# More seven-product quads in the down and output products of a float32 transformer block

## The chip, the core and the metric

The kernel runs on one core of a Trainium2 chip. Its time is the device time of one execution in microseconds; "before" is the median of three runs, 2025.66 us (2025.6 to 2025.71). The engines of the core run side by side, each with its own queue of instructions: TensorE (PE in the profile, its weight loads PEld), VectorE (DVE), ScalarE (ACT), GpSimd (POOL) and SyncE (SP), which here issues most loads. They wait for each other through semaphores.

## The reference

A block on 256 tokens of width 2048, in float32: a gated feed-forward block, a mixer (a recurrent branch and a pooling branch, gated and projected), and a second feed-forward block, each behind a norm and with a residual. What the change touches are the two down products and the mixer's last product:

```python
def _swiglu(x, w_gate, w_up, w_down):
    return (jax.nn.silu(x @ w_gate) * (x @ w_up)) @ w_down      # 256x2048, 2048x5632 twice, 5632x2048

f = _swiglu(_rmsnorm(h, ln_ffn1_pre[l]), ffn1_gate[l], ffn1_up[l], ffn1_down[l])
h = h + MACARON_WEIGHT * _rmsnorm(f, ln_ffn1_post[l])
...
m = jax.nn.sigmoid(g_a) * y_a + jax.nn.sigmoid(g_b) * y_b
return m @ w_out                                                 # 256x2048, 2048x2048
```

## The kernel before

**Products.** Every float32 operand is split into two halves of a faster type: ScalarE casts the value to its high half (H), VectorE subtracts that from the value and gets the low half (L). A product is then three matmuls, H·H, L·H and H·L (`mm3`, L311 to L315). A matmul takes 128 rows of the inner dimension, 128 tokens and 512 columns, and adds into a bank of PSUM. There are two halves of the tokens (h = 0, 1), so a plain step over one row block and one 512-column block is 2 x 3 matmuls. The down products have 44 row blocks and four column blocks, the output product 16 and four.

**Column pairs.** `seven` (L482) makes two neighbouring column blocks at once, f (first) and l (last). An order in letters says what TensorE does in turn: `f` or `l` is a pair, two row blocks against one column block, 12 matmuls (`pair`, L518); `q` is a quad, two row blocks against both column blocks (`quad`, L529). A quad uses Strassen's scheme in Winograd's form: seven products instead of eight, 21 matmuls. Its operands are sums of weight blocks (t13, t2 and t4, on VectorE, L548 to L560) and sums of activations (`sums`, L404, on VectorE and ScalarE; one set serves four row blocks, thus two quads, and is kept for both column pairs). The four weight operands of a quad are two raw ones and two sums; each is cast on ScalarE and has its low half made on VectorE (L562 to L573). When the last quad of a pair is done, its partial results are merged (`merge`, L622: a copy on ScalarE and four adds on VectorE, then one for each half of f, L653, and of l, L665). With `trail`, the last 16 row blocks of the pair's l column are done by halves of the tokens (`by_half`, L385), so that the first half is finished early.

**Buffers.** The weight halves go round in a ring of five buffers each (`WS_BUFS`), raw weights in four (`W32_BUFS`) or in the 33 general units of 4 KB a partition that also hold activations and sums. Four PSUM banks serve f and l, four the products that a quad keeps apart (p1, p5, p6, p7).

**Order.** For the two feed-forward blocks and the output product the order of work is made by a planner in the kernel (`Plan`, L87). TensorE's steps stand in the order of the letters, each at a planned time; every other operation is a node with a cost, a due time worked back from what needs it (L139 to L147), and buffers that it takes and gives back. `solve` (L134) puts the nodes into one sequence by a list scheduling with modelled costs, and `run` (L261) writes them out in it, as each engine's own order, under `manual_schedule` for TensorE, ScalarE, VectorE and SyncE. GpSimd is not in that list; there a scheduler of the framework decides. GpSimd issues the small transfers that carry the activations of the gate and up stage over from its layout to the next one (`carry`, L893; 16 transfers for each of the 11 blocks), the gains, the residual's loads and stores. `fetch` (L356) is the load, cast and low half of a pair.

The orders of the down products (`DOWN`, for columns 0 and 1, then 2 and 3), of the output product (`OUT`: column 0 plain, 1 and 2 as a pair, 3 plain) and of the gate and up products (`GATE_UP`, per block) are L45 to L48.

Of the kernel before, what the change touches and what calls it, by code (L numbers as in the profile page):

```python
# [17 lines left out]
P = 128  # L18
# [68 lines left out]
class Plan:  # L87
# [46 lines left out]
    def solve(s):  # L134
        succ = {n: [] for n in s.nodes}
        for n in s.nodes:
            for d in n.deps:
                succ[d].append(n)
        for n in reversed(s.nodes):  # L139
            for m in succ[n]:  # L140
                if n.eng == "PE":
                    break
                v = m.due - n.dur - (n.lat + (EARLY if m.eng == "PE" else 0.0)
                                     if m.eng != n.eng else 0.0)
                n.due = v if n.due is None else min(n.due, v)
            if n.due is None:
                n.due = n.born + LATEST  # L147
# [67 lines left out]
class Block:  # L215
# [139 lines left out]

    def fetch(s, w, k, c0, keep, hold=False):  # L356

        p, x = s.plan, {}
        src = Tok("w32", "unit")
        dst = [Tok("unit"), Tok("unit")] if hold else [Tok("ring")]  # L360

        def load():
            x["w"] = s.get_w(w, k, 2, c0, 512, own=src.of == "unit")

        def cast():
            x["v"], x["H"], x["L"] = s.halves_of(x["w"], hold)
            s.nc.scalar.copy(x["H"], x["v"])  # L367

        def low():
            s.nc.vector.tensor_tensor(out=x["L"], in0=x["v"], in1=x["H"].bitcast(F32),  # L370
                                      op=ALU.subtract)
            keep([(k + i, x["H"][:, i], x["L"][:, i]) for i in range(2)])
        n = p.op("SP", 0.4, load, take=[src], size=0.52, chain="SP")
        n = p.op("ACT", cost("ACT", 1024), cast, [n], take=dst, chain="cast")
        return p.op("DVE", cost("DVE", 1024), low, [n], rel=[src]), dst
# [28 lines left out]
    def sums(s, T, Td, j, out, own=None, nq=2, used=()):  # L404
# [25 lines left out]
        def parts():  # L430

            for n_ in ("sH", "sL"):
                if j % 2 == 0:
                    own["12" + n_] = s.unit((P, 2, 2, 2, P), F32R, n_)
                if j == 0:
                    own["4" + n_] = s.unit((P, 4, 2, P), F32R, n_)
# [3 lines left out]
            f = tt["f"]  # L440
            tt["p"] = [([u[:, j % 2] for u in s12], f[:, :2]),
                       ([u[:, j] for u in s4], f[:, 3]), (s3, f[:, 2])]
            for (H, _), v in tt["p"]:
# [38 lines left out]
    def seven(s, wf, cf, wl, cl, at, dep, KT, need, sm, order, ev_f, ev_l, used, trail=0):  # L482
# [34 lines left out]

        def pair(k, w, c0, b):  # L518
            low, dst = s.fetch(w, k, c0, keep)

# [8 lines left out]
        def quad(q):  # L529
# [40 lines left out]
            def low(n_, m):  # L570
# [3 lines left out]
            ld = [p.op("SP", 0.4, lambda m=m: get(m), take=([ka], [kb], (), ())[m], size=0.26,  # L574
                       chain="SP") for m in range(4)]

# [58 lines left out]
        for c in order:  # L635
            if c == "q":
                last["q"] = quad(nq)
                nq += 1
                if nq == n:
                    merge(last["q"])  # L640
                    if "f" in m:
                        close_f()
                continue
            w_ = (wf, cf) if c == "f" else (wl, cl)
            last[c] = pair(next(ks[c]), *w_, c)
            left[c] = left.get(c, 0) + 1
# [207 lines left out]
    def carry_steps(s, T1, T, x32=None):  # L854
# [3 lines left out]

        def move():
            if x32 is None:  # L860
                x[0] = s.unit((P, 4, 2, 4, 32), F32, "x32")
            src = s.blocks(T1[0])
            for i in range(4):
                for q in range(4):
# [19 lines left out]
        return move, high, low  # L884

    def carry_now(s, T1, T, x32):
        move, high, low = s.carry_steps(T1, T, x32)
        move()
# [3 lines left out]

    def carry(s, T1, T, turned, k1):  # L893

        p = s.plan
        move, high, low = s.carry_steps(T1, T)
        kx, kT = Tok("unit"), [Tok("unit"), Tok("unit")]
        n = p.op("POOL", 10.0, move, turned, [kx], [k1], chain="carry", spare=2, lat=8.0)
        hs = []
        for h in range(2):  # L900
            hs.append(p.op("ACT", cost("ACT", 512), lambda h=h: high(h), [n] + hs,
                           kT if h == 0 else (), chain="high",
                           spare=KEEP))
        for h in range(2):
            n = p.op("DVE", cost("DVE", 512), lambda h=h: low(h), [hs[h], n], (),
                     [kx] if h else ())
# [35 lines left out]
    def ffn(s, wg, wu, wd, uT, rs, gpost, resid, emit, reload, xs=None):  # L942
        nc = s.nc
        hT, sm = [], [None] * 8
        at = s.T_at(uT)
# [40 lines left out]
        def carry(b, turned, k1):  # L986
            n, k = s.carry(T1[b], hT, turned, k1)
            hTd.append(n)
# [966 lines left out]
```

## Time and profile before

| | |
|---|---|
| Median of three runs | 2025.66 us |
| The profiled execution | 2025.32 us |
| Its span, first to last instruction | 2023.6 us |
| Granted TensorE clock | 0.998 |
| Read from memory | 396.69 MB, 200 GB/s over the span |

In order of time the span holds: gate and up products of the first feed-forward block until about 469 us, its down product to about 701, the mixer with the output product (about 1257 to 1323 for the pair and the trailing column), gate and up products of the second block to about 1783, its down product to about 2013, and the store of the last rows.

The page's section 1 gives busy time by engine; a busy TensorE means that a matmul is in flight, and matmuls overlap, so the distance from start to start is their cost and not the duration of one. The list of waits gives for an engine what ended its idle time before an instruction: total, number of times, longest. Rows of a timeline give the start, the time, the engine, the source line, the operation, out<-in, how many equal ones were merged, and in brackets the idle time before it.

### The profile page before, as it was taken

How to read it: one execution, taken by the hardware profiler on the slowest of the kernel's cores; microseconds unless marked ns; L12 is line 12 of the kernel's file. 1: busy time of each engine (PE TensorE's matmuls, PEld its weight loads, DVE VectorE, ACT ScalarE, POOL GpSimd, SP SyncE). 2: the span in 40 equal slices, each digit the busy share in tenths (PEclk: the TensorE clock that was granted, in tenths of full speed). 3: DMA queues.
4: the chain of work that ended last, by engine and by line, in shares of the span. 5: the costliest groups of instructions: out<-in, count | busy, mean ns of one | idle time of the engine just before them, and what ended most of it. 6: DMA issues, size and time to landing. Idle time of an engine off the chain costs nothing.

```text
span 2023.6 us, 28609 instructions
## 1 busy us (share of the span) xinstructions
PE 2008.3 (99%) x9987; PEld 1660.2 (82%) x9987; DVE 1774.4 (88%) x2344; ACT 1180.8 (58%) x1575; POOL 325.2 (16%) x673
## 2 busy tenths in 40 slices
PE   9999999999999999999999999999999999999997
PEld 7888888888888888888788788888888888888886
DVE  6999999999989857799689577779999999999896
ACT  7565665655655566685576434565566556566553
POOL 0111211121000123403220111011112111210000
PEclk9999999999999999999999999999999999999999
DMA  7757475577567677757456558756574755775674
GB/s 267 254 179 265 148 253 188 186 221 245 185 204 268 225 204 214 204 175 216 147 169 187 160 169 278 245 196 232 187 266 151 246 190 183 223 243 189 203 261 145
DMA packets 227098, 423.55 MB, mean 209 GB/s; under 512 B 24320, under 2 KB 27786, under 8 KB 226954
## 3 DMA queue, kind: packets, MB, share of 16 engines
q1 hardware_dynamic: 204393, 384.70, 58.5%
q0 software_dynamic: 22272, 36.51, 5.5%
q8 instruction: 78, 1.28, 0.3%
q10 hardware_dynamic: 288, 0.52, 0.1%
q14 instruction: 67, 0.54, 0.1%
HBM read 396.69 MB, written 8.39 MB: 200 GB/s over the span
## 4 chain that ended last, share of the span: by engine, by line
PE 98%; issue 1%; DVE 1%; ACT 0%; DMA 0%; DVEq 0%; POOLq 0%; POOL 0%; SPq 0%; ACTq 0%
PE mm L313 27%; PE mm L315 27%; PE mm L314 27%; PE ms L313 4%; PE ms L315 4%; PE ms L314 4%; PE tr L822 0%; PE pA L1673 0%; PE mc L790 0%; PE pU L1769 0%; DMA w<-in_ffn_gate_dram 0%; PE pSa L1781 0%; PE pY L1804 0%; DVE xL L840 0%; PE pT L1840 0%
## 5 line engine op out<-in xcount | busy, mean ns | idle before, releaser
L313 PE MATMUL mm<-wH,xH 128*128 128x512 f32 (+1 forms) x2184 | 851.5, 391 | 0.4 <-ACT xH L831 0.4
L315 PE MATMUL mm<-wH,xL 128*128 128x512 f32 (+1 forms) x2184 | 847.8, 388 | 1.6 <-DVE xL L840 1.6
L314 PE MATMUL mm<-wL,xH 128*128 128x512 f32 (+1 forms) x2184 | 847.5, 388 | 0.0
L367 ACT CAST wH<-w 128x1024 fp32r<-128x1024 f32 x333 | 346.8, 1053 | 239.7 <-PE mm L315 209.2
L315 PEld LDWEIGHTS mm<-wH,xL 128*128 128x128 f32 x2184 | 409.9, 188 | 87.5 <-DVE xL L840 3.2
L313 PEld LDWEIGHTS mm<-wH,xH 128*128 128x128 f32 x2184 | 410.0, 188 | 85.5 <-ACT xH L831 1.0
L314 PEld LDWEIGHTS mm<-wL,xH 128*128 128x128 f32 x2184 | 410.1, 188 | 82.3
L370 DVE TENSOR_TENSOR wL<-w,wH 128x1024 fp32r<-128x1024 f32 x333 | 396.9, 1217 | 39.5 <-ACT wH L367 36.5
L567 ACT CAST wH<-t 128x1024 fp32r<-128x1024 f32 x188 | 198.2, 1054 | 222.8 <-PE mm L315 156.5
L290 DVE TENSOR_TENSOR wL<-w,wH 128x1024 fp32r<-128x1024 f32 (+2 forms) x202 | 239.0, 1192 | 96.5 <-ACT wH L289 93.3
L289 ACT CAST wH<-w 128x1024 fp32r<-128x1024 f32 (+2 forms) x202 | 207.7, 1034 | 164.5 <-PE mm L315 142.9
L865 POOL DMA_DIRECT2D x<-T x352 | 172.5, 498 | 748.4 <-DVE T L848 394.9
L572 DVE TENSOR_TENSOR wL<-t,wH 128x1024 fp32r<-128x1024 f32 x188 | 225.5, 1217 | 14.1 <-ACT wH L567 13.9
L567 ACT CAST wH<-w 128x1024 fp32r<-128x1024 f32 (+1 forms) x188 | 153.6, 835 | 48.4 <-PE mm L315 40.3
L572 DVE TENSOR_TENSOR wL<-w,wH 128x1024 fp32r<-128x1024 f32 (+1 forms) x188 | 175.6, 950 | 2.4 <-ACT wH L567 2.4
L550 DVE TENSOR_TENSOR t<-w,w 128x1024 f32<-128x1024 f32 x94 | 114.4, 1217 | 0.7 <-DMA w<-in_ffn_down_dram 0.7
L313 PE MATMUL ms<-wH,sH 128*128 128x512 f32 x252 | 98.0, 389 | 0.0
L314 PE MATMUL ms<-wL,sH 128*128 128x512 f32 x252 | 98.0, 389 | 0.0
L315 PE MATMUL ms<-wH,sL 128*128 128x512 f32 x252 | 98.0, 389 | 0.0
L559 DVE TENSOR_TENSOR t<-w,t 128x512 f32<-128x512 f32 x94 | 64.8, 689 | 2.1
L555 DVE TENSOR_TENSOR t<-w,t 128x512 f32<-128x512 f32 x94 | 64.3, 684 | 0.8
L619 DVE TENSOR_TENSOR u<-ms,u 128x512 f32<-128x512 f32 x92 | 61.3, 685 | 1.6
(311 smaller groups left out, 2017.6 us busy)
## 6 DMA issues: line engine op xcount, KB each, us to landing
w<-in_w_in_dram SPq DMA_DIRECT2D x128, 512.0 KB
w<-in_ffn_down_dram SPq DMA_DIRECT2D x116, 512.0 KB
w<-in_ffn_up_dram SPq DMA_DIRECT2D x114, 512.0 KB
w<-in_ffn_gate_dram SPq DMA_DIRECT2D x112, 512.0 KB
w<-in_ffn_gate_dram SPq DMA_DIRECT2D x128, 256.0 KB
w<-in_ffn_up_dram SPq DMA_DIRECT2D x124, 256.0 KB
w<-in_ffn_down_dram SPq DMA_DIRECT2D x120, 256.0 KB
w<-in_w_out_dram SPq DMA_DIRECT2D x28, 512.0 KB
```

The costliest lines, as they stand in the source:

```text
L289: s.nc.scalar.copy(vH, v)
L290: s.nc.vector.tensor_tensor(out=vL, in0=v, in1=vH.bitcast(F32), op=ALU.subtract)
L313: nc.tensor.matmul(ps, aH, bH, start=start, stop=False)
L314: nc.tensor.matmul(ps, aH, bL, start=False, stop=False)
L315: nc.tensor.matmul(ps, aL, bH, start=False, stop=stop)
L367: s.nc.scalar.copy(x["H"], x["v"])
L370: s.nc.vector.tensor_tensor(out=x["L"], in0=x["v"], in1=x["H"].bitcast(F32), op=ALU.subtract)
L550: V.tensor_tensor(out=v["t13"], in0=v["a"], in1=v["b"][:, :1].to_broadcast([P, 2, 512]), op=ALU.subtract)
L559: V.tensor_tensor(out=v["t24"][:, 1], in0=v["b"][:, 1], in1=v["t24"][:, 0], op=ALU.subtract)
L567: nc.scalar.copy(H, src)
L572: V.tensor_tensor(out=L, in0=src, in1=H.bitcast(F32), op=ALU.subtract)
L865: nc.gpsimd.dma_start(out=x[0][q * 32:q * 32 + 32, i], in_=src[i * 32:i * 32 + 32, q])
```

## The change

Three lines of letters change: the first pair of a down product has eight quads instead of seven, one in f's part and seven among the l pairs; the last pair has ten instead of eight, and its f and l pairs alternate between them; the output product's pair has four instead of two. GpSimd is added to the engines whose order the planner writes out. The planner's model of transfers changes (a higher rate; GpSimd's transfers no longer share SyncE's line; a transfer's time counts in due times; loads are not planned more than 22 us ahead of their due time), and the carry's 16 transfers become four nodes of four with a longer modelled latency. `sums` lets a fifth set of activation sums have units of its own, and `sm` has room for it.

The diff also brings a second way to make low halves (a copy of the negated high half, and a transfer from memory that adds onto it). It is reached by letters in upper case in an order, of which there are none, and by blocks in `BY_DMA`, which is `range(0)`; so nothing of it is in the built program.

```diff
-DOWN = ((0, "fffffffffqffffqff" "lqlllqllqllqllqlllll", 0),
-        (2, "fffqffqffqffqffqffqf" "lqllqlll", TRAIL))
-OUT = ((0, "", 0), (1, "fffffqf" "lqlllll", 0), (3, "", TRAIL))
+DOWN = ((0, "fffffffffffqfff" "qllqllqllqllqllqllqll", 0),
+        (2, "fqflqfqflqfqflqfqflqfqfqff", TRAIL))
+OUT = ((0, "", 0), (1, "fffqfq" "qlqlll", 0), (3, "", TRAIL))
...
+BY_DMA = range(0)
...
-SOON, LATEST, BEFORE = 22.0, 12.0, 12.0
+SOON, FETCH, LATEST, BEFORE = 22.0, 22.0, 12.0, 12.0
 EARLY = 0.5
-RATE, LEAVE, LAND = 0.25, 1.05, 2.0
+RATE, LEAVE, LAND, ADD, MOVE = 0.28, 1.05, 2.0, 10.0, 12.0
...
         for n in reversed(s.nodes):
+            lat = max(n.lat, n.size and LEAVE + n.size / RATE + LAND)
...
-                v = m.due - n.dur - (n.lat + (EARLY if m.eng == "PE" else 0.0)
+                v = m.due - n.dur - (lat + (EARLY if m.eng == "PE" else 0.0)
...
-                line = max(n.free + LEAVE, line) + n.size / RATE
-                n.end = max(n.end, line + LAND)
+                start = max(n.free + LEAVE, line)
+                line = start + n.size / RATE
+                n.end = max(n.end, (line if n.eng == "SP" else n.free + LEAVE + n.size / RATE)
+                            + LAND)
...
-        with s.tc.manual_schedule(engines={E.PE, E.Activation, E.DVE, E.SP}):
+        with s.tc.manual_schedule(engines={E.PE, E.Activation, E.DVE, E.SP, E.Pool}):
...
-        n = p.op("SP", 0.4, load, take=[src], size=0.52, chain="SP")
+        n = p.op("SP", 0.4, load, take=[src], size=0.52, chain="SP", ahead=FETCH)
...
-                if j % 2 == 0:
+                if j > 3:
+                    u = s.unit((P, 4, 2, P), F32R, n_)
+                    own["12" + n_], own["4" + n_] = u[:, :2], u[:, 2]
+                elif j % 2 == 0:
...
-            kept = [Tok("unit") for _ in range(2 * (j % 2 == 0) + 2 * (j == 0))]
+            kept = [Tok("unit") for _ in range(2 * (j % 2 == 0 or j > 3) + 2 * (j == 0))]
...
-        n = p.op("POOL", 10.0, move, turned, [kx], [k1], chain="carry", spare=2, lat=8.0)
+        n = None
+        for i in range(4):
+            n = p.op("POOL", 2.5, lambda i=i: move(i), [*turned, n], [kx] if i == 0 else (),
+                     [k1] if i == 3 else (), chain="carry", spare=2, lat=MOVE)
...
-        hT, sm = [], [None] * 8
+        hT, sm = [], [None] * 12
```

More of the change, by code (lines that the diff above doesn't have):

```diff
@@ L354, in gemm_tok, with fetch @@
                 evac(h, pss[h])
[L356 to L358 removed]
+    def fetch(s, w, k, c0, keep, hold=False, by_dma=False):
+        nc, p, x = s.nc, s.plan, {}
         src = Tok("w32", "unit")
@@ L516, in keep, with pair @@
             ws.update((k, (wH, wL)) for k, wH, wL in tiles)
-        def pair(k, w, c0, b):
-            low, dst = s.fetch(w, k, c0, keep)
+        def pair(k, w, c0, b, by_dma):
+            low, dst = s.fetch(w, k, c0, keep, by_dma, by_dma)
             def do():
@@ L574, in quad @@
             ld = [p.op("SP", 0.4, lambda m=m: get(m), take=([ka], [kb], (), ())[m], size=0.26,
-                       chain="SP") for m in range(4)]
+                       chain="SP", ahead=FETCH) for m in range(4)]
             def half(n_, m, deps, rel):
@@ L643, in seven @@
                 continue
+            by_dma, c = c in "FL", c.lower()
             w_ = (wf, cf) if c == "f" else (wl, cl)
-            last[c] = pair(next(ks[c]), *w_, c)
+            last[c] = pair(next(ks[c]), *w_, c, by_dma)
             left[c] = left.get(c, 0) + 1
@@ L857, in carry_steps, with move @@
         x, own = [x32], []
-        def move():
-            if x32 is None:
+        def move(*part):
+            if x[0] is None:
                 x[0] = s.unit((P, 4, 2, 4, 32), F32, "x32")
             src = s.blocks(T1[0])
-            for i in range(4):
+            for i in part or range(4):
                 for q in range(4):
@@ L883, in low, with whole, minus, add @@
                                     in1=part(dH, h).bitcast(F32), op=ALU.subtract)
-        return move, high, low
+        def whole(h):
+            nc.scalar.copy(part(own[0][1].bitcast(F32), h), by_k(h))
+        def minus():
+            x[0] = x[0].rearrange("p i h k c -> p (i h k c)")
+            nc.scalar.activation(out=x[0], in_=own[0][0].rearrange("p k t -> p (k t)")
+                                 .bitcast(F32), func=AF.Copy, scale=-1.0)
+        def add():
+            nc.gpsimd.dma_start(out=own[0][1].rearrange("p k t -> p (k t)"), in_=x[0],
+                                accum_op=ALU.add)
+        return move, high, low, whole, minus, add
     def carry_now(s, T1, T, x32):
-        move, high, low = s.carry_steps(T1, T, x32)
+        move, high, low = s.carry_steps(T1, T, x32)[:3]
         move()
@@ L903, in carry @@
                            spare=KEEP))
+        if by_dma:
+            for h in range(2):
+                n = p.op("ACT", cost("ACT", 512), lambda h=h: whole(h), [n, *hs])
+            n = p.op("ACT", cost("ACT", 1024), minus, [n, *hs])
+            return p.op("POOL", 1.25, add, [n], (), [kx], size=0.94, lat=ADD), kT
         for h in range(2):
@@ L986, in carry @@
         def carry(b, turned, k1):
-            n, k = s.carry(T1[b], hT, turned, k1)
+            n, k = s.carry(T1[b], hT, turned, k1, b in BY_DMA)
             hTd.append(n)
```

27 lines of the change are left out of this document (19 added, 8 removed).

## The prediction

> **What bounds the kernel now.** I read the page's head first, then the list of what TensorE waited for, then busy time by stretch.
>
> ```profile
> span 2023.6 us, 28609 instructions
> ...
> PE 2008.3 (99%) x9987; PEld 1660.2 (82%) x9987; DVE 1774.4 (88%) x2344; ACT 1180.8 (58%) x1575; POOL 325.2 (16%) x673
> ...
> PE warm L698 <- POOL ident masks.py:199: 1.7, 1, 1.7
> PE mm L315 <- DVE xL L840: 1.6, 4, 0.5
> PE pS L1789 <- ACT R L1783: 0.7, 1, 0.7
> PE mm L313 <- ACT xH L831: 0.4, 2, 0.2
> ```
>
> TensorE is busy for 2008.3 of 2023.6 us. The four lines behind it are all its waits on other engines, 4.4 us together, and none has a weight operand (wH, wL) in it: every weight half comes in time. So the end moves only if TensorE gets fewer instructions, or if it begins to wait. The second depends on VectorE, which makes the low halves:
>
> ```profile
> 100.00:460.00 360.00, 360.00 (x1590) 298.10 (x1589) 356.38 (x409) 213.93 (x238) 70.44 (x144) 1.00 0.63 206
> 470.00:570.00 100.00, 100.00 (x443) 82.81 (x442) 96.92 (x121) 59.69 (x73) 7.81 (x16) 1.00 0.61 205
> 584.00:684.00 100.00, 100.00 (x443) 82.81 (x442) 88.19 (x98) 57.69 (x65) 3.25 (x6) 1.00 0.74 251
> 1256.00:1301.00 45.00, 45.00 (x200) 37.30 (x199) 36.43 (x40) 25.62 (x32) 2.63 (x5) 1.00 0.83 295
> 1301.00:1322.00 21.00, 21.00 (x103) 17.47 (x102) 16.05 (x29) 13.41 (x30) 2.80 (x5) 1.00 0.53 175
> ```
>
> After the length stand TensorE's matmuls, its weight loads, VectorE, ScalarE and GpSimd, each with its count, then the granted clock (1.00). The first row is the gate and up products of the first feed-forward block: VectorE is busy 356.38 of 360 us there, and TensorE still never stops. The next two are the first and the last column pair of its down product, where VectorE has 3.1 and 11.8 us in 100 left. The last two are the output product's pair and its trailing column. One matmul costs TensorE 360 / 1590 = 0.2264 us.
>
> **The change part by part.** *Quads.* A quad multiplies two row blocks by two column blocks in 7 products of 3 matmuls (21) in place of 24. Each down product goes from 7 + 8 to 8 + 10 quads, the output product from 2 to 4: 2 x 3 + 2 = 8 quads more, so 24 matmuls fewer, and the built program has just 24 fewer TensorE instructions. 24 x 0.2264 = 5.43 us, all on the path, since TensorE never stands still beside them.
>
> A quad costs VectorE more. One is seen here in full:
>
> ```profile
> 559.65 1.22 DVE L550 TENSOR_TENSOR t<-w,w 128x1024 f32<-128x1024 f32 x1
> 560.79 1.22 DVE L572 TENSOR_TENSOR wL<-w,wH 128x1024 fp32r<-128x1024 f32 x1
> 561.92 0.68 DVE L555 TENSOR_TENSOR t<-w,t 128x512 f32<-128x512 f32 x1
> 562.64 0.69 DVE L559 TENSOR_TENSOR t<-w,t 128x512 f32<-128x512 f32 x1
> 563.25 0.68 DVE L572 TENSOR_TENSOR wL<-w,wH 128x512 fp32r<-128x512 f32 x1
> 563.86 2.35 DVE L572 TENSOR_TENSOR wL<-t,wH 128x1024 fp32r<-128x1024 f32 x2
> ```
>
> Start to start, a full-width instruction takes 1.14 us, a half one 0.61, and the half one whose input the one before has just written 0.72. The seven take 1.14 + 1.13 + 0.72 + 0.61 + 0.61 + 2.27 = 6.5 us, against 2 x 1.14 = 2.3 us for the two plain low halves that they replace: 4.2 us more, 34 us over eight quads. ScalarE gains two casts a quad and SyncE loads the same bytes in four pieces for two; at 58% busy ScalarE hides that. All 34 us must fit beside TensorE, so I look at the three tight places.
>
> *Sums of the activations.* Both last pairs use a ninth and tenth quad, which need a fifth set, and the output product a second one. One set in the trace, with what surrounds it:
>
> ```profile
> 1243.79 1.22 DVE L416 TENSOR_TENSOR sx<-xH,xL 128x1024 f32<-128x1024 f32 x1
> ...
> 1246.66 0.41 DVE L423 SCALAR_TENSOR_TENSOR sf<-sx 128x256 f32<-128x256 f32 x1
> ...
> 1249.37 1.23 DVE L464 TENSOR_TENSOR sL<-sf,sH 128x1024 fp32r<-128x1024 f32 x1 [1.17 <-ACT sH L460]
> 1250.52 3.49 DVE L370 TENSOR_TENSOR wL<-w,wH 128x1024 fp32r<-128x1024 f32 x3
> 1257.12 1.37 DVE L1109 TENSOR_TENSOR fg<-mm,gb 128x512 f32<-128x512 f32 x2 [3.12 <-ACT junk L940]
> ```
>
> A set is 1.14, then 1.54 for the four small ones (1246.66 to about 1248.20, where the wait of 1.17 begins), then 1.15: 3.8 us.
>
> *Output product.* VectorE's second set of sums fills the 1.17 and 3.12 us that it waits now. Behind that the pair has 36.4 us of work in 45 now; two quads more make 36.4 + 8.4 = 44.8 us, while TensorE's 45 shrink by 6 x 0.2264 to 43.6. The 1.2 us that this lacks come out of the lead: by hand, with these pitches and the order of the built program, the low halves are done 2 to 3 us early at the first two quads, and 0.7 us early at the tightest, the third operand of the fourth. The trailing column has 5 us in 21 to recover. From this I take no stall; the bound above is 1.2 us plus a hand-over that is late by one cast (1.05 us, below): 2 us.
>
> *Boundary between the column pairs.* Now the first pair ends with five plain pairs behind its last quad; after the change with two, and a quad follows one pair into the next. The results of the old pair must leave their banks in that time:
>
> ```profile
> 572.12 2.73 DVE L619 TENSOR_TENSOR u<-ms,u 128x512 f32<-128x512 f32 x4
> 574.77 1.28 DVE L619 TENSOR_TENSOR u<-mm,u 128x512 f32<-128x512 f32 x2
> ...
> 585.46 1.28 DVE L666 TENSOR_TENSOR u<-mm,u 128x512 f32<-128x512 f32 x2
> ```
>
> The six adds take 3.85 us (572.12 to 575.97). Behind them stand the new quad's seven instructions with the two adds of the last row in their midst (6.5 + 1.2): 11.6 us from the first add to the fourth operand. TensorE, from the end of the last quad, has 24 + 12 + 16 matmuls before it reads that operand: 52 x 0.2264 = 11.8 us. The first add needs a bank that is complete three matmuls before that end, so it can begin about 0.4 us ahead: 0.6 us to spare. I take no stall; if the first add is held by ScalarE, 1.0 us late is 0.4 us lost, 2.1 us late is 1.5 lost, at each of two boundaries. The lateness comes from the first two of these rows (total, times, longest, in 480 to 700 us); the third is the cast (its mean, 1.05 us):
>
> ```profile
> ACT wH L567 <- PE mm L315: 39.9, 31, 2.1
> ACT wH L367 <- PE mm L315: 27.1, 30, 1.7
> ...
> L367 ACT CAST wH<-w 128x1024 fp32r<-128x1024 f32 x333 | 346.8, 1053 | 239.7 <-PE mm L315 209.2
> ```
>
> *The second pair itself.* Between the first pair's last quad and the first trailing block TensorE has 24 + 16 x 12 + 10 x 21 = 426 matmuls, 96.4 us. VectorE has 15 plain low halves (17.1), ten quads (65), one set of sums (3.8) and eight adds (5.1): 91 us. It is 94% busy, less than the 99% that the gate and up stretch bears. The scaling of the results is put into the trailing blocks, where a low half of 1.14 us faces 12 matmuls, 2.7 us.
>
> *GpSimd listed.* GpSimd's instructions now keep the planner's order; in the built program that is the same order as before, instruction for instruction. Splitting the carry into four nodes, and the planner's other rates and lead times, move VectorE's work around at the start of each gate and up stage and in the down products, and leave the mixer as it was. The amount there is unchanged. I cost it at nothing, hidden by the same lead; if the new order lost that, one late operand would cost what the waits' first lines show, 0.2 to 0.5 us. The half-finished paths behind an empty range and capital letters are never run.
>
> *Sum.* The profiled execution took 2025.32 us with a span of 2023.6; 2025.32 - 5.43 = 2019.9, span 2018.2. The median of the runs is 0.3 above that execution: 2025.66 - 5.43 = 2020.2 us.
>
> **The rivals.** *Short stalls at the tight places.* Two boundaries at 0.4 to 1.5 us and the output product at up to 2: 1 to 5 us given back, 2021.2 to 2025.2, typically 2022.8. For it: 0.6 and 0.7 us are thin. Against it: both counts charge VectorE for every instruction and TensorE for no hand-over, as in the gate and up stretch, which runs at 99% without a wait.
>
> *The ring of five buffers (slower).* A quad takes four of the five pairs of cast buffers, and the cast rows above show ScalarE waiting for TensorE to free one, 61 times in 220 us, so the ring is always full. A plain pair directly behind a quad gets its buffer only 21 matmuls, 4.75 us, before it is due; cast and low half take 1.05 + 1.22 plus hand-overs, some 2.5. The 2.2 us left bear two half-width instructions ahead in VectorE's queue, but not a full set of sums. If every quad of the two last pairs and of the output product (24) lost 0.7 us, 17 us would be lost: 2025.7 - 5.4 + 17 = 2037. It decides from 0.4 us a quad, (5.4 + 4.1) / 24. Against it: the gate and up orders have quads with one pair between them three times running, with this ring, and no wait in the list.
>
> *VectorE's instructions don't overlap (slower too).* If the added ones, most of which wait for something, took the 1.22 and 0.68 us shown as their durations, "f q f l q" would need 3 x 1.22 + 2 x 6.93 = 17.5 us against 78 matmuls, 17.7, and sums, adds and scaling (13 us a block) would find no room: 2 x 12 + 5 us lost, 2049. The rows speak against it: 1.14 us from start to start under a duration of 1.22. The Trainium skill ("VectorE: DVE Perf Modes", The DRAIN you can't avoid) has the next instruction wait until the pipe is empty, save one that nothing holds; by its rule each added one would cost its full duration, and the trace, with starts 0.08 us before the end, shows the exception at work here.
>
> *It does not do what it says.* For GpSimd this holds already; for the quads the count of matmuls excludes it.
>
> **How the numbers follow.** The full gain has 0.72, short stalls 0.18, the ring 0.07, no overlap 0.03. What a measurement of this kernel can tell from no change is 0.2%, 4.05 us, so faster means under 2021.6: the first case, and the lowest part of the second. Same: most of the second, 0.17. Slower: the last two, 0.10. Faster 0.73. The likeliest case by itself spans 2019.7 (one of the small waits of today gone) to 2021. The range is 2019.6 to 2023.4: it takes in the bounds of the tight places up to about 3.2 us of stall.
>
> **What would show it.** Right: 9963 TensorE instructions, 2406 on VectorE; the same four waits and no line with wL or wH; in the last pair VectorE at 92 to 97% with TensorE full; a span near 2018.2. The boundary step is wrong if a matmul of the first pair in the new column waits for an add (u), the output step if one waits for a low half of the last quad. The prediction fails if TensorE's waits for wL come to more than 1.4 us.

## The result and the profile after

The changed kernel takes 2021.57 us (median of 16 runs, 2021.02 to 2024.22), the kernel before 2025.70 beside it (16 runs, 2025.31 to 2027.37): 4.13 us less, a ratio of 0.998 with a 95% interval of 0.9973 to 0.9988. The profiled execution took 2021.54 us.

The head of the page after, and all of TensorE's waits on it (total, times, longest):

```profile
span 2019.8 us, 28704 instructions
...
PE 2003.4 (99%) x9963; PEld 1654.7 (82%) x9963; DVE 1815.6 (90%) x2406; ACT 1196.6 (59%) x1598; POOL 325.9 (16%) x673
...
PE warm L718 <- POOL ident masks.py:199: 1.7, 1, 1.7
PE mm L319 <- DVE xL L860: 1.6, 4, 0.5
PE tr L842 <- DMA x<-in_x_dram: 1.0, 1, 1.0
PE pS L1829 <- ACT R L1823: 0.7, 1, 0.7
PE mm L317 <- ACT xH L851: 0.4, 2, 0.2
```

The counts are the predicted ones (9963 and 2406), and no weight half is among the waits. One line is new, the load of x, 1.0 us at the very start. Busy time by stretch, the stretches and columns of the prediction:

```profile
100.00:460.00 360.00, 360.00 (x1589) 297.88 (x1588) 354.33 (x406) 213.77 (x239) 70.59 (x144) 1.00 0.64 206
470.00:570.00 100.00, 100.00 (x442) 82.78 (x442) 97.72 (x121) 59.84 (x73) 7.85 (x16) 1.00 0.63 209
584.00:684.00 100.00, 99.90 (x441) 82.32 (x441) 99.50 (x112) 61.91 (x69) 3.25 (x6) 1.00 0.78 269
1256.00:1301.00 45.00, 45.00 (x201) 37.24 (x200) 44.83 (x50) 29.70 (x37) 2.65 (x5) 1.00 0.84 303
1301.00:1322.00 21.00, 21.00 (x102) 17.50 (x101) 18.29 (x37) 12.58 (x30) 2.80 (x5) 1.00 0.48 152
```

VectorE went from 88.19 to 99.50 us in the second pair and from 36.43 to 44.83 in the output product's. TensorE has lost 0.10 us in one row only, the third. That is where to look, with a finer means than the list of waits: a matmul is in flight for 0.39 us while the next starts 0.2264 later, so a start that is late by less than some 0.16 us leaves no idle time, and later ones show less than they cost. What counts is the distance from start to start. TensorE behind the boundary between the column pairs (the first row is the matmul right behind the last quad), then a cast on ScalarE and VectorE there (start, time, engine, line, operation; in brackets the idle time before it):

```profile
578.84 0.39 PE L317 MATMUL mm<-wH,xH 128*128 128x512 f32 x1
...
589.05 0.40 PE L317 MATMUL ms<-wH,sH 128*128 128x512 f32 x1
589.56 0.50 PE L318 MATMUL ms<-wL,sH 128*128 128x512 f32 x1
589.89 0.40 PE L319 MATMUL ms<-wH,sL 128*128 128x512 f32 x1
```

```profile
574.33 1.05 ACT L371 CAST wH<-w 128x1024 fp32r<-128x1024 f32 x1 [1.67 <-PE mm L319]
```

```profile
575.41 3.72 DVE L381 TENSOR_TENSOR wL<-w,wH 128x1024 fp32r<-128x1024 f32 x3 [1.14 <-ACT wH L371]
579.05 2.73 DVE L638 TENSOR_TENSOR u<-ms,u 128x512 f32<-128x512 f32 x4
581.70 1.28 DVE L638 TENSOR_TENSOR u<-mm,u 128x512 f32<-128x512 f32 x2
582.90 1.21 DVE L569 TENSOR_TENSOR t<-w,w 128x1024 f32<-128x1024 f32 x1
...
586.49 1.28 DVE L686 TENSOR_TENSOR u<-mm,u 128x512 f32<-128x512 f32 x2
587.69 0.68 DVE L591 TENSOR_TENSOR wL<-w,wH 128x512 fp32r<-128x512 f32 x1
588.29 2.35 DVE L591 TENSOR_TENSOR wL<-t,wH 128x1024 fp32r<-128x1024 f32 x2
```

The matmul that reads the third operand's low half starts 0.51 us behind the one ahead of it, 0.28 late, and the next 0.33 behind that, 0.11 late: 0.38 us. That low half is the first of the last row's two; it ends at about 589.50, and the matmul starts 0.06 us later. The same stands at 1900.8 us in the second block. In the kernel before, no start is late there, in either block. Each gate and up stage has one smaller case of the kind (418.08 and 1729.38 us, 0.11 late).

The start of the work differs from trace to trace (the first quad begins between 107.0 and 109.5 us), so I measure from the first quad to the last matmul. In the kernel before:

```profile
107.02 0.39 PE L313 MATMUL ms<-wH,xH 128*128 128x512 f32 x1
...
2012.43 0.39 PE L315 MATMUL mm<-kH,xL 128*128 128x512 f32 x1
```

and in the changed one:

```profile
107.42 0.39 PE L317 MATMUL ms<-wH,xH 128*128 128x512 f32 x1
...
2008.63 0.39 PE L319 MATMUL mm<-kH,xL 128*128 128x512 f32 x1
```

1905.41 against 1901.21 us: 4.20 less. Of the 5.43 us of the matmuls that were left out, 2 x 0.38 went at the boundaries and 2 x 0.11 in the gate and up stages; 0.25 us is spread over distances too small to be put to a place.

### The profile page after: what moved, and what is told of

It reads as the page before. It is cut to its first block, busy times and chain, and to the rows that moved or that the text cites. A ratio compares the mean times of both kernels' runs of the same rounds, so it can differ in the third digit from the quotient of the medians.

```text
span 2019.8 us, 28704 instructions
## 1 busy us (share of the span) xinstructions
PE 2003.4 (99%) x9963; PEld 1654.7 (82%) x9963; DVE 1815.6 (90%) x2406; ACT 1196.6 (59%) x1598; POOL 325.9 (16%) x673
## 4 chain that ended last, share of the span: by engine, by line
PE 97%; DVE 1%; issue 1%; ACT 0%; DMA 0%; DVEq 0%; POOLq 0%; POOL 0%; SPq 0%; ACTq 0%
PE mm L317 27%; PE mm L319 26%; PE mm L318 26%; PE ms L318 5%; PE ms L319 5%; PE ms L317 5%; PE tr L842 0%; PE pA L1713 0%; DVE u L638 0%; PE mc L810 0%; PE pU L1809 0%; DMA w<-in_ffn_gate_dram 0%; PE pSa L1821 0%; PE pY L1844 0%; DVE xL L860 0%
## 5 line engine op out<-in xcount | busy, mean ns | idle before, releaser
L317 PE MATMUL mm<-wH,xH 128*128 128x512 f32 (+1 forms) x2136 | 832.9, 391 | 0.4 <-ACT xH L851 0.4
L319 PE MATMUL mm<-wH,xL 128*128 128x512 f32 (+1 forms) x2136 | 829.1, 388 | 1.6 <-DVE xL L860 1.6
L318 PE MATMUL mm<-wL,xH 128*128 128x512 f32 (+1 forms) x2136 | 828.8, 388 | 0.0
L317 PEld LDWEIGHTS mm<-wH,xH 128*128 128x128 f32 x2136 | 400.8, 188 | 83.7 <-ACT xH L851 1.0
L371 ACT CAST wH<-w 128x1024 fp32r<-128x1024 f32 x317 | 330.7, 1054 | 223.6 <-PE mm L319 198.7
L381 DVE TENSOR_TENSOR wL<-w,wH 128x1024 fp32r<-128x1024 f32 x317 | 377.7, 1217 | 22.9 <-ACT wH L371 20.6
L586 ACT CAST wH<-t 128x1024 fp32r<-128x1024 f32 x204 | 215.2, 1055 | 223.5 <-PE mm L319 117.4
L591 DVE TENSOR_TENSOR wL<-t,wH 128x1024 fp32r<-128x1024 f32 x204 | 242.7, 1214 | 1.7 <-ACT wH L586 1.7
L586 ACT CAST wH<-w 128x1024 fp32r<-128x1024 f32 x204 | 165.4, 834 | 53.6 <-PE mm L319 31.5
L591 DVE TENSOR_TENSOR wL<-w,wH 128x1024 fp32r<-128x1024 f32 x204 | 191.1, 949 | 0.0
L569 DVE TENSOR_TENSOR t<-w,w 128x1024 f32<-128x1024 f32 x102 | 123.8, 1214 | 0.0
L578 DVE TENSOR_TENSOR t<-w,t 128x512 f32<-128x512 f32 x102 | 70.3, 689 | 2.2
L574 DVE TENSOR_TENSOR t<-w,t 128x512 f32<-128x512 f32 x102 | 69.9, 685 | 1.1
L638 DVE TENSOR_TENSOR u<-ms,u 128x512 f32<-128x512 f32 x92 | 61.1, 684 | 1.4
```

Of the source, the lines that this page charges most:

```text
L317: nc.tensor.matmul(ps, aH, bH, start=start, stop=False)
L318: nc.tensor.matmul(ps, aH, bL, start=False, stop=False)
L319: nc.tensor.matmul(ps, aL, bH, start=False, stop=stop)
L569: V.tensor_tensor(out=v["t13"], in0=v["a"], in1=v["b"][:, :1].to_broadcast([P, 2, 512]), op=ALU.subtract)
L578: V.tensor_tensor(out=v["t24"][:, 1], in0=v["b"][:, 1], in1=v["t24"][:, 0], op=ALU.subtract)
L586: nc.scalar.copy(H, src)
```

## The experiments

My theory at the outset, called "counted stalls" in the expectations, was the sum just above: the 5.43 us of the matmuls, less the stalls that the starts show. Each kernel was timed beside the kernel before, whose medians lay between 2025.56 and 2025.96 us. "First quad to last matmul" and "mixer" (first pV to last pT matmul) come from each profiled execution, worked out as above.

| Kernel | TensorE instructions | Median, us | First quad to last matmul | Mixer |
|---|---|---|---|---|
| before | 9987 | 2025.70 | 1905.4 | 330.9 |
| changed | 9963 | 2021.57 | 1901.2 | 330.9 |
| x1 planner only | 9987 | 2030.80 | 1911.0 | 334.5 |
| x2 longer tail | 9963 | 2025.20 | 1904.9 | 334.5 |
| x3 sixth buffer | 9963 | 2076.08 | 1956.6 | 375.6 |
| x4 eleven quads | 9957 | 2035.82 | 1915.4 | 330.9 |
| x5 down only | 9969 | 2022.81 | 1902.5 | 330.9 |
| x6 tail, taken early | 9963 | 2023.79 | 1902.9 | 330.9 |
| x7 old numbers | 9963 | 2021.61 | 1901.2 | 330.9 |
| x8 planner only, same mixer | 9987 | 2026.18 | 1905.6 | 330.9 |
| x9 nine and nine | 9963 | 2032.74 | 1912.0 | 330.9 |
| x10 nine and ten | 9957 | 2030.92 | 1910.8 | 330.9 |
| x11 one add less | 9963 | 2021.82 | 1900.4 | 330.9 |
| x12 first quad later | 9963 | 2021.47 | 1900.4 | 330.9 |

### The planner's part alone (x1, x8)

x1 has the old letters in the changed kernel:

```diff
-DOWN = ((0, "fffffffffffqfff" "qllqllqllqllqllqllqll", 0),
-        (2, "fqflqfqflqfqflqfqflqfqfqff", TRAIL))
-OUT = ((0, "", 0), (1, "fffqfq" "qlqlll", 0), (3, "", TRAIL))
+DOWN = ((0, "fffffffffqffffqff" "lqlllqllqllqllqlllll", 0),
+        (2, "fffqffqffqffqffqffqf" "lqllqlll", TRAIL))
+OUT = ((0, "", 0), (1, "fffffqf" "lqlllll", 0), (3, "", TRAIL))
```

> The changed kernel with the three old orders of letters put back: no quad is added, and only the planner's new numbers, the carry in four nodes and GpSimd in the list are left. 9987 TensorE instructions. Theory 'counted stalls' (of the 5.43 us, 0.38 is lost at each of two boundaries, 0.11 at one late operand in each gate and up stage, and the 0.4 us by which the first product starts later is chance of the one profiled execution): no stall at the boundaries, the two late operands (0.1 us each, near 418 and 1730 us) are here too, and the time is 2025.66 + 0.2 = 2025.9. Rival 'the listing and the numbers cost the start' (0.4 us are lost before the first product, systematically): 2026.1 to 2026.3, and the first product starts 0.4 us later than in the kernel before. Rival 'each quad costs TensorE more than its 21 matmuls': 2025.7, nothing lost here.

Measured: 2030.80 us, ratio 1.0025 (1.0015 to 1.0035), 5.2 us slower than the kernel before, timed beside it (2025.56); no theory had that. The mixer takes 3.6 us more, although no line of the mixer was edited. The first and the last row of the mixer on TensorE in the changed kernel (the last of the ten merged instructions starts 0.24 us behind the row's start, here as in x2 below):

```profile
862.79 0.27 PE L1650 MATMUL pV<-ident,zv 128*128 128x128 f32 x1
...
1193.47 0.46 PE L1880 MATMUL pT<-ident,R 64*64 64x64 f32 x10
```

x1 and x2 (below) take the same longer time there. In x2, the two rows, and the waits of TensorE between 863 and 1202 us:

```profile
862.82 0.27 PE L1650 MATMUL pV<-ident,zv 128*128 128x128 f32 x1
...
1197.12 0.46 PE L1880 MATMUL pT<-ident,R 64*64 64x64 f32 x10
```

```profile
PE pA L1713 <- DVE R L1689: 1.3, 2, 1.1
PE pB L1732 <- DVE R L1724: 1.1, 2, 0.8
PE pS L1829 <- ACT R L1823: 0.7, 1, 0.7
PE mm L317 <- ACT sgb L1349: 0.6, 1, 0.6
```

In the changed kernel only the line of pS is left of these four. The mixer isn't in the planner's sequence; its order on VectorE and ScalarE is made by the framework's scheduler, and in the built programs of x1 and x2 it is another than in the kernel before and in the changed one, with the same instructions. So an edit to the first block can swap 3.6 us in or out of a stage that it doesn't touch. All other variants but x3 have the changed kernel's mixer order.

x8 is x1 with the carry as one node again, which brings the old mixer order back:

```diff
-        for i in range(4):
-            n = p.op("POOL", 2.5, lambda i=i: move(i), [*turned, n], [kx] if i == 0 else (),
-                     [k1] if i == 3 else (), chain="carry", spare=2, lat=MOVE)
+        n = p.op("POOL", 10.0, move, turned, [kx], [k1], chain="carry", spare=2, lat=8.0)
```

> x1 (old orders of letters, the planner's new numbers) with the carry as one node again, by which the mixer's order on VectorE and ScalarE is again that of the kernel before. 9987 TensorE instructions. Theory 'x1's 5.1 us are the mixer's order (3.7 us between 863 and 1201 us) and 1.4 us of late low halves at the end of the second block': 2030.8 - 3.7 = 2027.1, with the mixer's stage as long as in the kernel before. Rival 'the numbers themselves slow the mixer': 2030.5 to 2031. Rival 'everything of x1 came from the carry's four nodes': 2025.7.

2026.18 us, ratio 1.0 (0.9991 to 1.0009), mixer 330.9. The 3.6 us are the mixer's order. The late low halves that x1 has near 2002 to 2006 us (1.5 us from start to start) are gone as well, which I had expected to stay. So the third theory held: x1's loss came with the carry's four nodes. The two late operands of the gate and up stages are in x1 and not in x8, so they too come with these nodes.

### Price of the output product's quads (x5), old planner numbers (x7)

x5 takes back `OUT` alone, to the line of x1's diff.

> The changed kernel with the output product's old order (two quads for four): 9969 TensorE instructions, the mixer's order on every engine as in the changed kernel. Theory 'counted stalls': the two quads of the output product are worth their 6 matmuls and no stall, so 2021.57 + 1.36 = 2022.9, with the two boundary stalls of the down products as before. Rival 'the output product's two quads give back what they save' (its spare of 0.5 us is too thin): 2021.6 or less.

2022.81 us, 1.24 above the changed kernel, 1.29 by the traces (1902.50 against 1901.21), for 6 matmuls worth 1.36. The output product's quads pay nearly in full, and the 0.38 us at the boundaries are here too.

x7 puts three of the numbers back:

```diff
-            lat = max(n.lat, n.size and LEAVE + n.size / RATE + LAND)
+            lat = n.lat
...
-        n = p.op("SP", 0.4, load, take=[src], size=0.52, chain="SP", ahead=FETCH)
+        n = p.op("SP", 0.4, load, take=[src], size=0.52, chain="SP")
```

with the other load (L594) likewise, and the carry as in x8.

> The changed kernel with three of the planner's new numbers put back: loads may again be issued any time ahead, due times leave the transfer out, and the carry is one node. New orders, 9963 TensorE instructions, the mixer's order as in the changed kernel. Theory 'counted stalls': the late operand in each gate and up stage (0.115 us) goes, the boundaries stay: 2021.57 - 0.23 = 2021.3. Rival 'the numbers keep the loads in time': waits for wH after a load (DMA) appear, 2022 or more. Rival 'the numbers cost the start': first product 0.4 us earlier, 2020.9.

2021.61 us: unchanged. The late operands of the gate and up stages are gone and the boundary lost only 0.18 us a block, but a low half near the end of the product is late now: 0.11 us in the first block, 0.57 in the second. What was saved came back elsewhere.

### Is it the amount of VectorE's work? (x4, x10, x9)

x4 has an eleventh quad in the second pair:

```diff
-        (2, "fqflqfqflqfqflqfqflqfqfqff", TRAIL))
+        (2, "fqflqfqfqlqfqfqlqfqfqfqff", TRAIL))
```

> The changed kernel with eleven quads for ten in the second pair of each down product (6 matmuls fewer, 9957 TensorE instructions, 1.36 us). It tests the step that VectorE's work in that pair is hidden at 94%. The eleventh quad needs a sixth set of sums: 14 plain low halves (16.0), eleven quads (71.5), two sets (7.6) and eight adds (5.1) are 100.2 us against 423 matmuls, 95.8 us. Theory 'VectorE's amount is the next bound': 4.4 us too much, of which a lead of 2 to 3 us hides a part; 1.4 to 2.4 us lost in each of two pairs, 2021.57 - 1.36 + 2.8 to 4.8 = 2023.0 to 2025.0, with waits for wL in the second pair. Rival 'there is still room' (the trailing block's slack is drawn forward): 2020.2, no such wait.

2035.82 us, far above the 2023 to 2025 expected. The waits of TensorE in x4 between 480 and 700 us:

```profile
PE mm L318 <- DVE wL L381: 3.3, 2, 1.9
PE ms L318 <- DVE wL L591: 1.4, 4, 0.5
PE mm L318 <- DVE wL L591: 0.5, 2, 0.3
```

From start to start TensorE loses 7.9 us in the block, 0.4 of it at the boundary as before. A quad and its set of sums are 4.2 + 3.8 = 8.0 us of VectorE. VectorE has no idle time over 0.15 us in x4 between 575 and 695 us. So nearly all of the addition came onto TensorE, and no lead hid it.

x10 puts a ninth quad into the first pair:

```diff
-DOWN = ((0, "fffffffffffqfff" "qllqllqllqllqllqllqll", 0),
+DOWN = ((0, "fffffffffqffqff" "qllqllqllqllqlqllqll", 0),
```

> The changed kernel with a ninth quad in the first pair of each down product and ten in the second: 6 TensorE instructions fewer (9957, 1.36 us), the mixer's order the same. VectorE does 4.2 us more in the first pair, and the fifth set of sums moves there from the second pair, whose work falls by 3.8 us to 87. Theory 'VectorE's amount in the second pair decides': the first pair has the room, the boundary stall stays at 0.4 or less, 2021.57 - 1.36 = 2020.2 (2019.5 if the boundary stalls go). Rival 'a further quad in the down product costs what x4's did' (7.9 us a block): 2035. Rival 'the boundary takes it all': 4 us late there, 2 x 4 - 1.36 = 2028.

2030.92 us, between the two rivals. Busy time from 475 to 595 us, first in the changed kernel, then in x10:

```profile
475.00:595.00 120.00, 119.90 (x529) 98.90 (x528) 116.30 (x141) 70.16 (x88) 7.85 (x16) 1.00 0.60 198
```

```profile
475.00:595.00 120.00, 116.55 (x507) 94.14 (x505) 119.26 (x151) 69.53 (x89) 7.83 (x16) 1.00 0.57 187
```

The changed kernel leaves VectorE 3.7 us in this stretch; quad and set need 8.0. In x10 VectorE is full, and TensorE loses 5.3 us in the block by its starts. The prediction's row for the first pair shows 3.1 us left in 100 as well; x10's expectation, that this pair has the room, overlooked it.

x9 has nine quads in each pair:

```diff
+DOWN = ((0, "fffffffffqffqff" "qlqllqllqllqllqllqll", 0),
+        (2, "fqflqfqflqfqflqfqflqfqfflff", TRAIL))
```

The ninth set of sums is written partly over the activations of row block 18, which the second pair of this variant still multiplies in plain form, so these products change; the instructions and their order are what they would be.

> The changed kernel with one quad moved from the second pair of each down product to the first (9 and 9 for 8 and 10): 9963 TensorE instructions as in the changed kernel, the mixer's order the same. The set of sums that the ninth quad needs (3.8 us of VectorE) moves into the first pair with it, so the second pair's VectorE work falls from 91 to about 84 us. Theory 'VectorE's amount in the second pair decides, and the boundary stall and the stalls at the pair's end in x6 are one shortage that changes its place': no wait for a low half from the boundary to the end of the product, 2021.57 - 0.77 = 2020.8. Rival 'the boundary by itself': its order (q l l, then f q) is unchanged, so 0.38 stays at each, 2021.6. Rival 'the first pair can't carry it': waits for wL ahead of 589 us, 2022 or more.

2032.74 us: 5.6 us a block lost from 533 to 594 us, all in the first pair and at the boundary, nothing behind it. The third theory was right, the first pair can't carry a ninth quad. The second pair, relieved, says nothing here, since the stalls ahead of it had given VectorE time.

### The boundary itself (x2, x6, x12, x11)

x2 and x6 move a plain pair behind the last quad of the first pair, x2 from its middle, x6 from its beginning:

```diff
-DOWN = ((0, "fffffffffffqfff" "qllqllqllqllqllqllqll", 0),
+DOWN = ((0, "fffffffffffqfff" "qllqllqlqllqllqllqlll", 0),    # x2
+DOWN = ((0, "fffffffffffqfff" "qlqllqllqllqllqllqlll", 0),    # x6
```

> The changed kernel, same quads (9963 TensorE instructions), but the first pair's order ends q l l l: one plain pair is moved from the middle behind the last quad, so that TensorE has 12 matmuls (2.72 us) more before it reads the next pair's first quad, and VectorE 1.14 us more to do. Theory 'counted stalls': both boundary stalls (0.38 us each) go, 2021.57 - 0.77 = 2020.8, and no matmul of the new pair's first quad waits for a low half. Rival 'each quad costs more than its matmuls': nothing moves, 2021.6. Rival 'VectorE's amount in the first pair is the bound' (two quads with one plain pair between them come out of its lead): the stall moves into the first pair, 2021.6 or a little more.

> As x2, a plain pair moved behind the last quad of the first pair (... q l l l), but taken from behind that pair's first last-column quad (q l q l l ...), which leaves the mixer's order on every engine as in the changed kernel; 9963 TensorE instructions. Theory 'counted stalls': both boundary stalls go, 2021.57 - 0.77 = 2020.8. Rival, from x2's trace (a wait for wL of 0.75 us inside the second pair of the first block): a part of it comes back there, 2021.1 to 2021.6. Rival 'x2 was slow because of its letters and not because of the mixer's order': 2025.

x2 took 2025.20 us, 3.6 above the changed kernel, which is the size of the mixer's other order. At its boundary no start is late, but 0.75 us are lost at 637.9 us in the first block, and 0.11 in the second. x6 has the old mixer and took 2023.79 us: the boundary stalls went, and 1.2 us a block came back, worse than the first two theories said and better than the third. VectorE in x6 behind the boundary (between the two rows lie 16 us of work), then TensorE's wait near the end of the product:

```profile
605.63 1.22 DVE L381 TENSOR_TENSOR wL<-w,wH 128x1024 fp32r<-128x1024 f32 x1 [0.61 <-ACT wH L371]
...
623.31 2.54 DVE L381 TENSOR_TENSOR wL<-w,wH 128x1024 fp32r<-128x1024 f32 x2 [1.00 <-ACT wH L371]
```

```profile
685.89 0.50 PE L318 MATMUL mm<-kL,xH 128*128 128x512 f32 x1 [0.66 <-DVE kL L381]
```

VectorE stands still for 1.6 us, for casts that themselves wait for a matmul of TensorE to free a buffer (ScalarE's cast ahead of the second row waited 1.66 us so). Behind that it has no idle time over 0.15 us until the late matmul. The changed kernel has none in the whole stretch. By this trace, VectorE's lead ends where the ring is full, and what it can't do then is missing 60 us later. x12, which comes next, gives VectorE as much time at the boundary and it does not idle, so the order of the letters matters there as well; why was not pursued.

x12 puts one plain pair ahead of the new pair's first quad, and keeps all behind the third quad:

```diff
-        (2, "fqflqfqflqfqflqfqflqfqfqff", TRAIL))
+        (2, "ffqlqfqflqfqflqfqflqfqfqff", TRAIL))
```

> The changed kernel with the second pair's order beginning f f q l q f q f l for f q f l q f q f l: the new pair's first quad comes 12 matmuls (2.72 us) later, all behind its third quad is as before. 9963 TensorE instructions, the mixer's order as in the changed kernel. Theory 'VectorE's amount over the whole second pair lacks 0.4 us': the stall leaves the boundary and comes back at the second quad or behind it, 0.3 to 0.5 us a block, 2021.6. Rival 'only the boundary is tight': no stall in its place, 2020.8. Rival 'x6's mechanism (VectorE idles at the full ring)': 0.8 us a block more than now, 2023.

No start is late any more from the boundary to the end of the product, in either block. The same stretch as above, x12's VectorE at the boundary, and its first quad and last matmul:

```profile
577.52 4.86 DVE L381 TENSOR_TENSOR wL<-w,wH 128x1024 fp32r<-128x1024 f32 x4 [1.14 <-ACT wH L371]
582.29 2.73 DVE L638 TENSOR_TENSOR u<-ms,u 128x512 f32<-128x512 f32 x4
...
591.53 2.35 DVE L591 TENSOR_TENSOR wL<-t,wH 128x1024 fp32r<-128x1024 f32 x2
```

```profile
109.51 0.39 PE L317 MATMUL ms<-wH,xH 128*128 128x512 f32 x1
...
2009.88 0.39 PE L319 MATMUL mm<-kH,xL 128*128 128x512 f32 x1
```

1900.37 us against 1901.21: 0.84 less, where 0.77 was expected of "only the boundary is tight". The median, 2021.47 us (ratio 0.9977, 0.9967 to 0.9986), is 0.10 below the changed kernel's, and the intervals overlap; by the times alone the two can't be told apart. In the profiled execution x12's first quad came 2.1 us later than the changed kernel's; whether that is chance or belongs to x12 wasn't settled. That execution (2023.07 us) was the slowest of x12's ten, and the fastest took 2020.62, so executions of one program differ by more than this.

x11 takes VectorE work away at that place and touches nothing else:

```diff
-                            d = p.op("DVE", one, lambda h=h, i=i: add(i, f"f{h}", i),
+                            d = p.op("DVE", one, lambda h=h, i=i: (trail or KT < NKF or h == 0) and add(i, f"f{h}", i),
```

> The changed kernel with one VectorE instruction less at each boundary: of the two adds that bring the plain pairs' sum of the first column into its two results (L686), the second row half's is left out in the first pair of each down product, so that half of that column lacks its plain row blocks. 0.6 us of VectorE less between the old pair's results and the new quad's third operand; orders, TensorE's 9963 instructions and the mixer's order as in the changed kernel. In the changed kernel's trace VectorE has no idle time over 0.15 us from 575.4 to 683.7 us. Theory 'VectorE's amount over that stretch is what lacks 0.4 us': the boundary stalls go and nothing comes back behind, 2021.57 - 0.77 = 2020.8. Rival 'the casts that wait for a buffer, or a hand-over': they are untouched, 0.27 and 0.11 us stay at the boundary, 2021.6. Rival, as in x6, 'VectorE runs into the full ring, idles there and is late behind': the boundary stalls go, VectorE idles for 0.5 us or more between 600 and 625 us, and a wait for a low half comes up near the product's end, 2021.6 to 2023.8.

(In the trace the add that was left out is one of the two in the row "L638 u<-mm"; the expectation names the line of the last column's adds.) With 0.6 us of work less ahead of the third operand the boundary stalls are gone in both blocks and nothing comes back. Its first quad and last matmul:

```profile
107.80 0.39 PE L317 MATMUL ms<-wH,xH 128*128 128x512 f32 x1
...
2008.15 0.39 PE L319 MATMUL mm<-kH,xL 128*128 128x512 f32 x1
```

1900.35 us, 0.86 less. The median, 2021.82 us, again doesn't separate it. The 1.14 us of idle time ahead of the plain low halves are still there, so that wait alone doesn't make the stall; it takes it and the amount behind it together.

### A sixth pair of cast buffers (x3)

```diff
-W32_BUFS = 4
-WS_BUFS = 5
+W32_BUFS = 3
+WS_BUFS = 6
...
-NUNITS = 33
+NUNITS = 32
...
-UNITS = dict(ffn=25, out=22)
+UNITS = dict(ffn=24, out=21)
```

> The changed kernel with six pairs of cast buffers for five; one load buffer and one of the large buffers make room for it. Same orders, 9963 TensorE instructions. Theory 'counted stalls', in its reading that the plain low halves behind the last quad start late since their casts wait for a buffer that TensorE frees (VectorE idle for 1.14 us just ahead of them, at 574 us): with one buffer more that idle time shrinks or goes, the adds begin up to 0.6 us earlier, and the two boundary stalls go: 2020.8. Rival 'VectorE's amount between the last quad and the third operand is the bound': the idle time may go but the stall stays at 0.3 us or more, 2021.5. Should the load buffer that is missing cost something, waits for wH after a load show it and the time is above 2021.6.

2076.08 us. The mixer alone took 45 us longer: TensorE waited for VectorE there (16.0 and 12.0 us at the longest), and between 1031 and 1070 us the granted clock was 0.78. Which part of the edit did this isn't shown, and the time says nothing about the ring. What ScalarE waited for between 480 and 700 us, first in the changed kernel, then in x3:

```profile
ACT wH L371 <- PE mm L319: 25.7, 32, 1.7
ACT wH L586 <- PE mm L319: 19.0, 18, 2.1
...
ACT wH L586 <- DMA w<-in_ffn_down_dram: 4.7, 5, 2.8
```

```profile
ACT wH L586 <- DMA w<-in_ffn_down_dram: 19.8, 12, 4.1
...
ACT wH L371 <- PE mm L319: 5.5, 6, 1.7
...
ACT wH L586 <- PE mm L319: 3.2, 6, 1.5
```

The waits for a free cast buffer fell from 44.7 to 8.7 us, but loads came late in their place, and TensorE lost 5.5 us in the first block. A ring of six with all its load buffers was not run, so what the ring by itself is worth stays open.

## Why the prediction was right, and where it was off

The forecast was 2020.2 us with 2019.6 to 2023.4; 2021.57 lies inside, 1.4 above the forecast. The mechanism held: fewer matmuls on a TensorE that is always busy, worth 4.20 of the 5.43 us by the trace. But the likeliest case, no stall and 2019.7 to 2021 us at 0.72, did not come; the case of short stalls at 0.18 did. The boundary step failed, and VectorE's room in the second pair was smaller than counted. The span is 2019.8 us and not near 2018.2.

*Quads, minus 5.43 us.* Right: 24 instructions fewer, and x5 shows two quads at 1.24 to 1.29 of 1.36 us.

*VectorE's additions hidden beside TensorE.* Right in the outcome, by less than the text said. The second pair's VectorE came to 99.50 of 100 us where 92 to 97% was forecast. The prediction counted 15 plain low halves up to the first trailing block; from 578.9 to 675.6 us the trace has 19, so VectorE does four of the trailing block's ahead. It has no idle time over 0.15 us from 575.4 to 688 us, across pair and trailing block, so the 6% that the count left free were not spare. x4 and x10 show that the next quad's 8.0 us come through almost whole (7.5 us more in x4's first block, 4.9 in x10's, where 3.7 us were free). With the orders tried, eight and ten is as far as these pairs go; other orders of the same letters were not tried. The lead that the prediction trusted is short: in x6 it ends at the full ring.

*Output product, no stall.* Right: TensorE full in both rows, and x5's price.

*Boundary between the column pairs, 0.6 us to spare.* This step failed: 0.38 us was lost at each. Its amount was exact: from the first add at 579.05 to the end of the fourth low half at 588.29 + 2.35 = 590.64 are 11.6 us, as counted. Two other numbers weren't. The operand that comes tight is the third: it is ready 10.45 us after the first add and is read 46 matmuls, 10.4 us, after the last quad, which with the 0.4 us of lead leaves 0.4 us and not 0.6. And the adds didn't begin 0.4 us ahead of the last quad's end but 0.2 behind it (the matmul behind the quad starts at 578.84), because VectorE was still at the three plain low halves ahead of them, which had started late behind casts that waited for the ring. 0.4 - 0.6 is the 0.2 to 0.3 us that the matmul started late; the matmul behind it lost 0.11 more. The text's bound for adds that are held, "1.0 us late is 0.4 us lost", names the measured loss only by chance: they came 0.6 us late, for which it gives nothing, and VectorE's own queue held them, not ScalarE's copy. Nor did the sign that the prediction named for this step appear, a matmul that waits for an add; and the list of waits, its other sign, doesn't show the stall at all. x11 and x12 confirm the place, each by removing the stall; that the casts' wait is what made the adds late is read from the trace and was not tested by itself.

*GpSimd and the planner's numbers, nothing.* Right for the list: leaving GpSimd out of it gives the same program on every engine. The carry's four nodes cost 0.11 us in each gate and up stage (x7 and x8, with one node, are without it), where the prediction gave 0.2 to 0.5 us for one late operand. What the prediction did not see is a risk beside this: with the old letters the same four nodes turn the mixer's order, at 3.6 us (x1 against x8). The changed kernel happens to have the good one, as the prediction said of its built program; no rival named what the other would have cost.

*The rivals.* Short stalls is what came, with 1.0 us just at its lower end and under its typical 2.6. The ring of five buffers is a real limit, but as an end to VectorE's lead (x6), not as 0.7 us a quad. VectorE's instructions overlap as before: 2.35 us for two low halves of 1.22 us each.

x12 is the better order by its trace, by 0.84 us; its time doesn't show it yet.

## What to carry to other kernels

Where an engine feeds another through a short ring, its spare time can be saved up only as far as the ring holds it: compare the two engines' work over short stretches, and look at every operand of the tight step, not only the last. Before an experiment is read, see that the stages that it doesn't touch kept their order; a scheduler can change them for an edit elsewhere, and here that was as large as the effect. A list of waits hides lateness under the overlap of pipelined instructions; measure from start to start.

## What the runs showed of the hardware

A matmul that had to wait for its operand costs more than its wait: the trace has it in flight for 0.50 us and not 0.39, and the next one starts 0.33 to 0.34 us behind it instead of 0.2264. The row at 589.56 and the one behind it show this, and so does the one at 685.89 in x6 (the next start was at 686.23). Such a late hand-over thus costs about 0.11 us on top, even where the matmul itself starts only 0.01 us late, as the one ahead of 418.08 us does in the changed kernel. A few cases in other runs cost less, 0.06 to 0.10 us.
